# Attention rows in turns of two differential and two grouped-query rows, with the second map folded in by the ratio of the sums

## The chip, the cores and the metric

The program runs on one core of one Trainium2 chip. The metric is the device time of one execution in microseconds. The engines are TensorE (PE; its weight loads are shown as PEld), VectorE (DVE), ScalarE (ACT), GpSimd (POOL) and SyncE (SP). All DMAs of this kernel are issued from SP's queue. The 16 DMA engines of the core do the transfers, and also the transposes of 16-bit tiles (DMA_TRANSPOSE), which are called turns below.

## The reference, cut to what matters

One layer of a hybrid block over 2048 latent tokens and 256 context tokens, width 1024. Three mixers run side by side: pooling, differential attention (4 heads, two maps each) and grouped-query attention (8 heads of 64, two key/value groups of 4 heads). Queries are the 2048 latent tokens; keys and values are all 2304 tokens.

```
def _diff_core(q, k, v, lam):
    s = einsum('bqhcd,bkhcd->bhcqk', q, k) * (DIFF_HEAD_DIM ** -0.5)
    p = softmax(s, axis=-1)
    a = p[:, :, 0] - lam * p[:, :, 1]
    return einsum('bhqk,bkhe->bqhe', a, v)

def _diff_post(o, diff_subln, lam_init):
    o = _rmsnorm(o, diff_subln) * (1.0 - lam_init)

def _gqa_core(q, k, v):
    s = einsum('bqgrd,bkgd->bgrqk', q, k) * (GQA_HEAD_DIM ** -0.5)
    p = softmax(s, axis=-1)
    return einsum('bgrqk,bkgd->bqgrd', p, v)
```

Around it stand one input projection, gates (SiLU paths and sigmoid merges), branch projections and an output projection.

## The kernel before, in words

There are three stages. Stage 1 makes normalised tokens, projects queries, keys and values, and rounds them to pairs of f16 (a high part and what it leaves, a low part) in DRAM. Its fourth projection (the loop with `gating`) also loads the last third of `ada_w` through the `raw` tag and adds its products (`ada_product`, line 218), two per token tile. Stage 3 merges the branches and projects to the output.

Stage 2, which the change is about, has 256 score rows (line 710). A row is 128 queries of one map against all 2304 tokens. `score_row` issues ten matmuls in two PSUM tiles `sa` (1024 columns) and `sb` (1280), takes the maxima on VectorE (lines 759 to 761) and the exponentials on ScalarE with their sums (lines 764, 765). The PSUM tiles exist once, so the matmuls of the next row wait for the exponentials of this one. The first 128 rows are differential: for each head h and block j of 256 queries, halves o = 0, 1, and in each the maps c = 0, 1. The last 128 rows are grouped-query (gqa): 8 heads, 8 blocks, two halves.

What follows a row is put in two tables: `ahead` (issued before the scores of a slot) and `after` (issued behind them). For a pair of differential rows with the second at slot i: at i+1 the inverse sums, a GpSimd pass that scales the second map (`scale_second`, line 802), and VectorE's `combine` (line 806); at i+2 `high`, the f16 part on ScalarE, and `low`, the rest on VectorE (line 815). A gqa row does `high` (line 833) and `low` (line 838) at i+1. Each of them ends in `turn`: a DMA_TRANSPOSE of 128 x 2304 values into the tile `th` (line 786). Parts have four buffers, maps (`pt`) three, turned tiles four, for two steps at once. A step is a block of 256 queries; when both halves are turned, `diff_av` (54 matmuls of 256 columns) or `gqa_av` (36) multiplies it with the values, from the table `fills`: two rows after its last `low`.

PE's remaining time in a slot is filled with the gate projection (`gate_unit`, 24 matmuls of 512 columns for one 128 x 512 tile, 160 units). A planner at lines 928 to 960 gives each row the same PE time: it counts 1.95 for a row, 0.107 for an av matmul, 0.2135 for a gate matmul, and takes av work first, then gate matmuls, until the slot's goal is reached. Units 0 to 15 go out as they are, units 16 to 63 (SiLU paths) get a tanh on ScalarE and then the VectorE step of line 189, units 64 and up a tanh only. Gate weights come through the tag `raw` and are split on GpSimd (lines 158 to 163). Values are loaded in six parts and split on VectorE (lines 742, 744), one part in two rows as a rule. `diff_norm` makes the inverse norms of all four heads at slot 136.

The engines work in the order in which the program issues to them, SP included: a DMA that waits holds up those behind it.

## Time and profile before

| | us |
|---|---|
| median of 3 runs (lowest to highest) | 3084.66 (3082.51 to 3088.21) |
| the profiled execution | 3082.73 |
| its span, first to last instruction | 3080.9 |
| PE busy in the span | 2830.0 (92%) |
| DVE busy | 2312.8 (75%) |
| ACT busy | 1561.5 (51%) |
| POOL busy | 858.7 (28%) |
| stage 2, first to last row's first reduction | 652.6 to 2530.8 |

Busy shares are means over stages with different limits. Matmuls overlap and their ends are modelled, so a busy PE is not PE at its peak. In the list of groups a line has the source line, engine, operation, tiles and shapes, the count, the busy time and the mean of one, and after the last bar the idle time of the engine just before, with what ended it.

### The profile page before, as it was taken

The numbers are of one execution on the slowest core, as the hardware profiler recorded it, in microseconds if no ns is written. First come the engines' busy times: TensorE is split into PE (matmuls) and PEld (weight loads), VectorE is DVE, ScalarE is ACT, GpSimd is POOL, SyncE is SP. The second block draws the span as 40 slices with busy tenths as digits, with TensorE's granted clock in tenths as the row PEclk, the third lists the DMA queues.
The fourth block names the chain that finished last, engine by engine and source line by source line (L and its number), as shares of the span: only waits on it lengthen the run. The fifth ranks groups of instructions, "written<-read, shape, count | busy, mean of one in ns | idle before, by whom it ended". The sixth has DMA issues, their size and how long they took to land. (4 is left out here: it accounts for less than half of the span.)

```text
span 3080.9 us, 40994 instructions
## 1 busy us (share of the span) xinstructions
PE 2830.0 (92%) x15013; PEld 1656.3 (54%) x15013; DVE 2312.8 (75%) x2886; ACT 1561.5 (51%) x2038; POOL 858.7 (28%) x752
## 2 busy tenths in 40 slices
PE   6997887899999999999998998998999997999999
PEld 1543333645545545545555555555555554787787
DVE  3567885668988988988987887888788775756753
ACT  4722121236556556556666776777777772223221
POOL 0034453533332332332322010010010113434421
PEclk8999998999999999999999999999999998999999
DMA  6243552246666765666689999999999997677574
GB/s 238 103 123 100 140 144 62 64 109 138 149 142 132 149 145 128 154 137 146 145 178 174 200 196 199 196 195 197 203 197 198 196 193 218 209 253 250 201 256 150
DMA packets 1134266, 516.46 MB, mean 168 GB/s; under 512 B 985040, under 2 KB 1038704, under 8 KB 1134064
## 3 DMA queue, kind: packets, MB, share of 16 engines
q1 hardware_dynamic: 1134064, 513.84, 70.4%
q8 instruction: 118, 1.93, 0.2%
q14 instruction: 84, 0.69, 0.1%
HBM read 208.24 MB, written 78.97 MB: 93 GB/s over the span
## 5 line engine op out<-in xcount | busy, mean ns | idle before, releaser
L177 PE MATMUL gate<-hT,gws 128*128 128x512 f16 x3840 | 872.5, 381 | 0.0
L177 PEld LDWEIGHTS <-gws 128*128 128x128 f16 x3840 | 374.3, 98 | 421.7 <-issue 21.0
L764 ACT ACTIVATE pt<-sa,nm,escale 128x1024 f32<-128x1024 f32 x256 | 307.9, 1203 | 439.7 <-DVE nm L761 392.3
L756 PEld LDWEIGHTS <-qt 128*128 128x128 f16 x2560 | 249.9, 98 | 337.6 <-issue 52.2
L838 DVE SCALAR_TENSOR_TENSOR lo<-pt,nm,hi 128x2304 f16<-128x2304 f32 x128 | 339.0, 2649 | 101.2 <-DMA th<-lo 92.9
L491 PE MATMUL qkv<-wt,hT 128*128 128x512 f16 (+1 forms) x1920 | 400.1, 365 | 0.0
L760 DVE TENSOR_REDUCE nm<-sb 128x1 f32<-128x1280 f32 x256 | 379.0, 1480 | 0.6 <-PE sb L756 0.6
L833 ACT ACTIVATE hi<-pt,nm 128x2304 f16<-128x2304 f32 x128 | 283.5, 2215 | 177.9 <-DMA th<-hi 121.9
L878 PE MATMUL av<-th,vt 128*128 128x256 f16 x2304 | 287.9, 284 | 85.9 <-DMA th<-lo 46.7
L759 DVE TENSOR_REDUCE nm<-sa 128x1 f32<-128x1024 f32 x256 | 311.1, 1215 | 73.3 <-PE sa L756 72.5
L765 ACT ACTIVATE pt<-sb,nm,escale 128x1280 f32<-128x1280 f32 x256 | 360.4, 1408 | 0.0
L756 PE MATMUL sb<-kt,qt 128*128 128x512 f16 (+1 forms) x1536 | 319.2, 344 | 13.7 <-ACT pt L765 12.9
L878 PEld LDWEIGHTS <-vt 128*128 128x128 f16 x2304 | 229.6, 102 | 140.5 <-issue 63.6
L162 POOL TENSOR_SCALAR gws<-gw 128x512 f16<-128x512 f32 x76 | 76.5, 1006 | 812.4 <-PE gate L177 808.0
L491 PEld LDWEIGHTS <-hT 128*128 128x128 f16 x1920 | 191.4, 100 | 182.2 <-issue 18.2
L756 PE MATMUL sa<-kt,qt 128*128 128x512 f16 x1024 | 262.9, 379 | 12.8 <-ACT pt L764 5.7
L802 POOL TENSOR_SCALAR pt<-pt,nm,neglam 128x2304 f32<-128x2304 f32 x64 | 144.7, 2261 | 459.7 <-DVE nm L771 437.4
L1125 PE MATMUL br<-bt,wt 128*128 128x512 f32 x1152 | 268.2, 393 | 2.4 <-DVE wt L980 2.4
L1125 PEld LDWEIGHTS br<-bt,wt 128*128 128x128 f32 x1152 | 217.4, 189 | 52.0 <-DVE wt L980 3.5
L852 PE MATMUL av<-th,vt 128*128 128x256 f16 x1728 | 198.9, 273 | 1.1 <-ACT ms L868 1.1
L1157 PE MATMUL out<-y,wt 128*128 128x512 f32 x768 | 187.3, 403 | 9.9 <-DVE wt L980 4.7
L378 ACT ACTIVATE sp<-tpq 128x512 f16<-128x512 f32 (+1 forms) x68 | 34.8, 512 | 313.0 <-PE tpq L376 310.4
(195 smaller groups left out, 3323.0 us busy)
## 6 DMA issues: line engine op xcount, KB each, us to landing
tD<-gt SPq DMA_DIRECT2D x96, 256.0 KB, 2.4
wr<-in_w_br SPq DMA_DIRECT2D x32, 768.0 KB
ld<-tD SPq DMA_DIRECT2D x96, 256.0 KB, 4.6
scan<-in_w_gate SPq DMA_DIRECT2D x40, 512.0 KB, 3.9
gw<-in_w_gate SPq DMA_DIRECT2D x80, 256.0 KB, 4.0
qt<-qD SPq DMA_DIRECT2D x256, 64.0 KB, 2.7
wr<-in_w_out SPq DMA_DIRECT2D x32, 512.0 KB, 4.3
sgD<-gt SPq DMA_DIRECT2D x48, 256.0 KB, 2.4
```

The source lines that it names most:

```text
L177: nc.tensor.matmul(ps, lhsT=w[:, b, k, :], rhs=hT[k][:, a, c * CH:(c + 1) * CH], start=(n == 0), stop=(n == 3 * KT - 1))
L491: nc.tensor.matmul(ps[:, :width], lhsT=tokens_of(t, k, a), rhs=wt[k][:, b, :width], start=(n == 0), stop=(n == 3 * KT - 1))
L756: nc.tensor.matmul(dst, lhsT=qt[:, s, o * P:(o + 1) * P], rhs=kt[:, k0:k1], start=(s == 0), stop=(s == 1))
L759: nc.vector.tensor_reduce(out=nm[:, 0:1], in_=sa, axis=AX.X, op=ALU.max, negate=True)
L760: nc.vector.tensor_reduce(out=nm[:, 1:2], in_=sb, axis=AX.X, op=ALU.max, negate=True)
L764: nc.scalar.activation(out=pt[:, :SA], in_=sa, func=AF.Exp, scale=escale[:, m:m + 1], bias=nm[:, 0:1], accum_out=nm[:, 2:3])
L765: nc.scalar.activation(out=pt[:, SA:], in_=sb, func=AF.Exp, scale=escale[:, m:m + 1], bias=nm[:, 0:1], accum_out=nm[:, 3:4])
L833: nc.scalar.activation(out=box["hi"], in_=pt, func=AF.Copy, scale=nm[:, 2:3])
L838: nc.vector.scalar_tensor_tensor(out=lo, in0=pt, scalar=nm[:, 2:3], in1=box["hi"], op0=ALU.mult, op1=ALU.subtract)
L852: nc.tensor.matmul(ps[:, :256], lhsT=vt[:, k, v, :], rhs=pts[a][:, k, :], start=(n == 0), stop=(n == 3 * NKT - 1))
L878: nc.tensor.matmul(ps[:, :256], lhsT=vt[:, k, :, :].rearrange("p a d -> p (a d)"), rhs=pts[a][:, k, :], start=(n == 0), stop=(n == 2 * NKT ...
L1125: nc.tensor.matmul(ps, lhsT=wb[:, a, 4 * br + k, :], rhs=branch_tile(c, br, k)[:, b], start=(m == 0), stop=(m == 11))
```

## The change

The rows run in turns: two differential rows, two gqa rows, and so on, so that eight rows hold one differential step and two gqa steps. `high` and `low` of a gqa row stand two slots after its scores, and its av work at i+4. The second map is no longer scaled on GpSimd: `combine` multiplies it by (sum of the first) / (sum of the second) x (-lambda) while it adds the first map, and the common inverse sum is applied in `high` and `low`. Values of a differential head have one buffer, gqa values two; both are loaded two parts per slot from the third row of a head on (or two slots before a group). `diff_norm` runs once for each head, twelve rows into the next head, and for the last head behind all rows. The `raw` tag has 4 buffers instead of 5, maps 4 instead of 3, query tiles 5 instead of 4; the ada products of stage 1 follow their loads by one token tile instead of two. Forced av work is now counted by the planner.

```diff
     def raw(name):
-        return shp.tile([P, 512], F32, name=name, tag="raw", bufs=5)
+        return shp.tile([P, 512], F32, name=name, tag="raw", bufs=4)
...
-                if gating and u < 10:
+                if gating and u < 9:
...
-                        if m >= 4:
-                            ada_product(gps[m % 2], (m - 4) // 2, ada_raws.pop(0))
-                elif gating and u == 10:
+                        if m >= 2:
+                            ada_product(gps[m % 2], (m - 2) // 2, ada_raws.pop(0))
+                elif gating and u == 9:
                     rws = ada_rows(gps)
...
-        rows = [("d", h, j, o, c) for h in range(4) for j in range(8) for o in range(2) for c in range(2)]
-        rows += [("g", h, j, o, 0) for h in range(8) for j in range(8) for o in range(2)]
+
+        rows = []
+        for n in range(32):
+            for o in range(2):
+                rows += [("d", n // 8, n % 8, o, c) for c in range(2)]
+                m = 2 * n + o
+                rows += [("g", m // 8, m % 8, p, 0) for p in range(2)]
...
             if part == 0:
-                values[key] = sp.tile([P, NKT, 2, n], F16, name="vt", tag="vt", bufs=2)
+
+                use_up((key[0], key[1] - 1))
+                values[key] = sp.tile([P, NKT, 2, n], F16, name="vt", tag="vt" + key[0], bufs=1 if key[0] == "d" else 2)
...
-            pt = sp.tile([P, NTOK], F32, name="pt", tag="pt", bufs=3)
+            pt = sp.tile([P, NTOK], F32, name="pt", tag="pt", bufs=4)
...
-            nc.vector.reciprocal(out=nm[:, 2:3], in_=nm[:, 2:3])
+            nc.vector.reciprocal(out=nm[:, 3:4], in_=nm[:, 2:3])
...
-            def scale_second():
+            def ratio():
+
                 inverse_sum(nm, lscale[:, 0:1])
-                nc.gpsimd.tensor_scalar(out=pt, in0=pt, scalar1=nm[:, 2:3], scalar2=neglam[:, 0:1], op0=ALU.mult,
-                                        op1=ALU.mult)
+                nc.vector.tensor_scalar(out=nm[:, 2:3], in0=nm[:, 3:4], scalar1=n0[:, 2:3], scalar2=neglam[:, 0:1],
+                                        op0=ALU.mult, op1=ALU.mult)
 
             def combine():
-                nc.vector.scalar_tensor_tensor(out=p0, in0=p0, scalar=n0[:, 2:3], in1=pt, op0=ALU.mult, op1=ALU.add)
+                nc.vector.scalar_tensor_tensor(out=p0, in0=pt, scalar=nm[:, 2:3], in1=p0, op0=ALU.mult, op1=ALU.add)
...
-                nc.scalar.activation(out=box["hi"], in_=p0, func=AF.Copy)
+                nc.scalar.activation(out=box["hi"], in_=p0, func=AF.Copy, scale=n0[:, 3:4])
...
-                nc.vector.tensor_tensor(out=lo, in0=p0, in1=box["hi"], op=ALU.subtract)
+                nc.vector.scalar_tensor_tensor(out=lo, in0=p0, scalar=n0[:, 3:4], in1=box["hi"], op0=ALU.mult,
+                                               op1=ALU.subtract)
...
-            at(ahead, i + 1, high)
-            at(after, i + 1, low)
+            at(ahead, i + 2, high)
+            at(after, i + 2, low)
             if o == 1:
-                at(fills, i + 3, lambda: gqa_av(h, j, values["g", h // 4], turned.pop(step)))
+                at(fills, i + 4, lambda: (("g", h // 4), gqa_av(h, j, values["g", h // 4], turned.pop(step))))
...
-        def diff_norm():
-
-            rr = sp.tile([P, 64], F32, name="rr", tag="rr", bufs=1)
-            for h in range(4):
-                dma(out=rr[:, h * 16:(h + 1) * 16], in_=msD[h].rearrange("o (p t) -> p (o t)", p=P))
+        def diff_norm(h):
+
+            rr = sp.tile([P, 16], F32, name="rr", tag="rr", bufs=2)
+            dma(out=rr, in_=msD[h].rearrange("o (p t) -> p (o t)", p=P))
...
+                if kind == "d":
+                    at(ahead, i - 3, lambda h=h, c=c: load_keys((h, c), h, c))
+                    if c == 0:
+                        for p in range(6):
+                            at(ahead, i + 3 + p // 2, lambda h=h, p=p: load_part(("d", h), vD, h * P, P, 0, p))
+                        if h:
+                            at(ahead, i + 12, lambda h=h: split_later.append(diff_norm(h - 1)))
+                elif h % 4 == 0:
+                    at(ahead, i - 2, lambda g=h // 4: load_keys(("g", g), 4, g))
                     for p in range(6):
+                        at(ahead, i - 2 + p // 2, lambda g=h // 4, p=p: load_part(("g", g), gvD, g * 64, 64, 1, p))
+        at(ahead, NR + 5, lambda: split_later.append(diff_norm(3)))
```

## Rows read from the trace of the kernel before

**Rows 1.** The page: span, and the busy tenths of 40 slices for DMA.

```profile
span 3080.9 us, 40994 instructions
DMA  6243552246666765666689999999999997677574
```

**Rows 2.** Busy time by stretch: us, each engine's busy us and instructions, clock, DMA share.

```profile
762.30:1337.80 575.50, 555.60 (x3122) 300.73 (x3121) 510.54 (x564) 337.53 (x450) 192.51 (x138) 1.00 0.65 142
1397.10:1560.30 163.20, 163.20 (x935) 90.19 (x934) 144.94 (x157) 101.20 (x135) 57.29 (x43) 1.00 0.65 146
1688.70:2530.80 842.10, 768.81 (x4534) 445.46 (x4533) 678.46 (x736) 601.84 (x670) 103.73 (x89) 0.98 1.01 197
```

**Rows 3.** The same stretches for line 759 alone: the count is that of rows.

```profile
762.30:1337.80 575.50, 96.61 (x80) 1.00 0.65 142
1397.10:1560.30 163.20, 29.33 (x24) 1.00 0.65 146
1688.70:2530.80 842.10, 135.26 (x112) 0.98 1.01 197
```

**Rows 4.** Instructions on tile sa: ns min/median/max, first and last start in us.

```profile
L759 DVE TENSOR_REDUCE nm<-sa x256: 1203/1223/1226, 652.6 to 2530.8; 128x1 f32<-128x1024 f32 x128
```

**Rows 5.** Groups of PE in the stretch 1397.1 to 1560.3.

```profile
L177 PE MATMUL gate<-hT,gws 128*128 128x512 f16 x360 | 80.7, 379 | 0.0
L852 PE MATMUL av<-th,vt 128*128 128x256 f16 x323 | 37.2, 273 | 0.0
L756 PE MATMUL sb<-kt,qt 128*128 128x512 f16 (+1 forms) x144 | 30.0, 343 | 0.0
L756 PE MATMUL sa<-kt,qt 128*128 128x512 f16 x96 | 24.6, 379 | 0.0
L866 PE MATMUL ms<-o,ones 128*1 128x256 f32 x12 | 3.6, 377 | 0.0
```

**Rows 6.** The chain of waits, pieces by time: start us, us, what.

```profile
2188.87 4.75 PE gate L177 x22
...
2195.56 3.71 PE av L878 x35
```

**Rows 7.** Groups of PE, DVE and ACT in the gqa stretch 1688.7 to 2530.8.

```profile
L177 PE MATMUL gate<-hT,gws 128*128 128x512 f16 x1404 | 322.8, 380 | 0.0
L878 PE MATMUL av<-th,vt 128*128 128x256 f16 x2016 | 248.9, 281 | 71.4 <-DMA th<-lo 43.9 <-DMA th<-hi 23.5 <-DVE nm L761 1.9
...
L838 DVE SCALAR_TENSOR_TENSOR lo<-pt,nm,hi 128x2304 f16<-128x2304 f32 x111 | 294.3, 2652 | 86.0 <-DMA th<-lo 79.8 <-ACT hi L833 5.8
...
L833 ACT ACTIVATE hi<-pt,nm 128x2304 f16<-128x2304 f32 x111 | 245.9, 2215 | 155.9 <-DMA th<-hi 105.1 <-DVE nm L771 39.4 <-DVE nm L761 3.2
```

**Rows 8.** Groups of DVE in the stretch with line 189, 762.3 to 1337.8.

```profile
L806 DVE SCALAR_TENSOR_TENSOR pt<-pt,nm 128x2304 f32<-128x2304 f32 x40 | 105.6, 2641 | 2.5 <-POOL pt L802 2.5
...
L189 DVE SCALAR_TENSOR_TENSOR gt<-gt,gate 128x512 f32<-128x512 f32 x48 | 32.9, 686 | 42.2 <-ACT gt L186 42.2
...
L769 DVE TENSOR_SCALAR nm<-nm,lscale 128x1 f32<-128x1 f32 x80 | 21.5, 269 | 7.6 <-ACT pt L765 7.6
```

**Rows 9.** The hardware DMA queue: 1688.7 to 2530.8, then 1397.1 to 1560.3.

```profile
q1 hardware_dynamic: 554098, 165.36, 100.4%
...
q1 hardware_dynamic: 66268, 23.74, 64.9%
```

**Rows 10.** Instructions on tile th: issue of a turn on SP, and time to landing.

```profile
L786 SPq DMA_TRANSPOSE th<-lo x192: 2389/2748/3739, 679.5 to 2549.2; - x192
...
DMA to landing us min/median/max: 4.5/4.8/6.4
```

**Rows 11.** Timeline behind the last row: start us, us, what.

```profile
2559.25 17.00 PE L177 MATMUL gate<-hT,gws 128*128 128x512 f16 x78
```

**Rows 12.** Timeline in stage 1: an ada load, and the next product on PE.

```profile
456.26 0.89 SPq L667 DMA_DIRECT2D aw<-in_ada_w  x2
...
460.32 1.88 PE L218 MATMUL ada<-aw,cct 128*2 128x512 f32 x4
```

**Rows 13.** All splits of values on VectorE, ns min/median/max.

```profile
L744 DVE SCALAR_TENSOR_TENSOR vt<-vr,vscale,vt x36: 417/619/1559, 662.8 to 2026.1; 128x384 f16<-128x384 f32 x24, 128x192 f16<-128x192 f32 x12
```

More of the change, by code (lines that the diff above doesn't have):

```diff
@@ L725, in load_queries @@
         def load_queries(key, pair, half, j):
-            qt = queries[key] = sp.tile([P, 2, 256], F16, name="qt", tag="qt", bufs=4)
+            qt = queries[key] = sp.tile([P, 2, 256], F16, name="qt", tag="qt", bufs=5)
             for o in range(2):
@@ L778, in turn @@
                 while a == 0 and len(live) == 2:
-                    for _ in avs[0]:
-                        pass
-                    avs.pop(0)
+                    finish_first()
                 if a == 0:
@@ L822, in diff_row @@
             if o == 1:
-                at(fills, i + 4, lambda: diff_av(h, j, values["d", h], turned.pop(step)))
+                at(fills, i + 4, lambda: (("d", h), diff_av(h, j, values["d", h], turned.pop(step))))
         def gqa_row(i, h, j, o):
@@ L866, in square_sum @@
                 nc.tensor.matmul(pm[0:1, :256], lhsT=ones, rhs=o2, start=True, stop=True)
-                ms = sp.tile([1, 256], F32, name="ms", tag="ms", bufs=1)
+                ms = sp.tile([1, 256], F32, name="ms", tag="o2", bufs=2)
                 nc.scalar.activation(out=ms, in_=pm[0:1, :256], func=AF.Copy)
@@ L898, in rest @@
                 nc.vector.tensor_scalar(out=rr, in0=rr, scalar1=1.0 / P, scalar2=EPS, op0=ALU.mult, op1=ALU.add)
-                nc.gpsimd.tensor_tensor(out=rr, in0=rr, in1=mhalf, op=ALU.pow)
-                for h in range(4):
-                    dma(out=rD[h].rearrange("o (p t) -> p (o t)", p=P), in_=rr[:, h * 16:(h + 1) * 16])
-            return rest
-        fills, first = {}, {}
+                nc.gpsimd.tensor_tensor(out=rr, in0=rr, in1=mhalf[:, :16], op=ALU.pow)
+                dma(out=rD[h].rearrange("o (p t) -> p (o t)", p=P), in_=rr)
@@ L906, in block_kernel, with load_part @@
+            return rest
+        fills, first, split_later = {}, {}, []
+        def load_part(key, src, c0, n, m, p):
+            split_later.append(load_values(key, src, c0, n, m, p))
         for i, (kind, h, j, o, c) in enumerate(rows):
-            if kind == "d":
-                if j == 0 and o == 0:
-                    at(ahead, i - (5 if c == 0 else 1) if h else 0, lambda h=h, c=c: load_keys((h, c), h, c))
-                if o == 0:
-                    at(ahead, i - 3, lambda h=h, c=c, j=j: load_queries((h, j, c), h, c, j))
-                if j == 0 and o == 0 and c == 0:
-                    for p in range(6):
-                        at(ahead, i + p - 1 if h == 0 else i - 14 + 2 * p, lambda h=h, p=p: split_later.append(
-                            load_values(("d", h), vD, h * P, P, 0, p)))
-            else:
-                g = h // 4
-                if h % 4 == 0 and j == 0 and o == 0:
-                    at(ahead, i - 20, lambda g=g: load_keys(("g", g), 4, g))
-                    for p in range(6):
-                        at(ahead, i - 16 + 2 * p, lambda g=g, p=p: split_later.append(
-                            load_values(("g", g), gvD, g * 64, 64, 1, p)))
-                if o == 0:
-                    at(ahead, i - 4, lambda h=h, j=j: load_queries((4 + h, j, 0), 4 + h // 2, h % 2, j))
@@ L925, in block_kernel @@
-        split_later = []
-        at(ahead, 136, lambda: split_later.append(diff_norm()))
+            if o == 0:
+                pair = (h, c) if kind == "d" else (4 + h // 2, h % 2)
+                key = (h, j, c) if kind == "d" else (4 + h, j, 0)
+                at(ahead, i - 3, lambda key=key, pair=pair, j=j: load_queries(key, *pair, j))
+            if j == 0 and o == 0:
+                if kind == "d":
[7 more added lines that the diff above has]
+                    at(ahead, i - 2, lambda g=h // 4: load_keys(("g", g), 4, g))
+                    for p in range(6):
+                        at(ahead, i - 2 + p // 2, lambda g=h // 4, p=p: load_part(("g", g), gvD, g * 64, 64, 1, p))
@@ L928, in block_kernel @@
+        at(ahead, NR + 5, lambda: split_later.append(diff_norm(3)))
         total = (160 - HEAD_UNITS - TAIL_UNITS) * 24 * 0.2135 + NR * 1.95 + 32 * (54 * 0.107 + 0.45) + 64 * 36 * 0.107
-        spent = 0.0
+        spent = [0.0]
         row_now = [0]
-        for i in range(NR + 5):
+        for i in range(NR + 7):
             row_now[0] = i
@@ L945, in block_kernel @@
                     gqa_row(i, h, j, o)
-                spent += 1.95
+                spent[0] += 1.95
             for f in todo + after.pop(i, []):
                 f()
-            goal = total * (i + 1) / NR if i < NR else spent + 24 * 0.2135 * (i < NR + 3)
-            while avs and spent < goal:
-                t = next(avs[0], None)
+            goal = total * (i + 1) / NR if i < NR else spent[0] + 24 * 0.2135 * (i < NR + 4)
+            while avs and spent[0] < goal:
+                t = next(avs[0][1], None)
                 if t is None:
@@ L954, in block_kernel @@
                 else:
-                    spent += t
-            while spent < goal:
+                    spent[0] += t
+            while spent[0] < goal:
                 t = next(dense, None)
@@ L959, in block_kernel @@
                     break
-                spent += t
-        for a in avs:
+                spent[0] += t
+        for _, a in avs:
             for _ in a:
                 pass
+        assert not (ahead or after or fills)
     if stop == 2:
```

12 lines of the change are left out of this document (9 added, 3 removed).

## The prediction

> **What bounds the kernel now.** I began with the page's forty slices. The DMA line stands at 9 from about 1600 us to 2540 us and at 5 to 7 in the 900 us before that [rows 1]. Both halves are the attention stage, of 256 score rows, 128 differential rows and then 128 grouped-query (gqa) rows. So the next view was busy time by stretch, with the count of the row's first reduction in the same stretches as a row counter [rows 2, 3]. It gives three paces: 575.5/80 = 7.19 us a row while gate tiles with the extra VectorE step (line 189) are made, 163.2/24 = 6.80 us for differential rows without that step, and 842.1/111 = 7.59 us for gqa rows. All 255 steps from the first row's reduction to the last take 2530.8 - 652.6 = 1878.2 us [rows 4].
>
> Is 6.80 a floor? PE is busy in all 163.2 us of its stretch, but the matmuls overlap, so that alone says little. I took the pitch instead: 22 gate matmuls in a row are 4.75 us, 0.216 each, and 35 av matmuls 3.71 us, 0.106 each [rows 6]. With the counts of the stretch [rows 5] this is 360 x 0.216 + 323 x 0.106 + 96 x 0.216 + (96 x 0.216 + 48 x 0.106) + 3.6 = 162 of 163.2 us. PE streams without a hole there; 6.80 is its floor. The same sum for the gqa stretch, with the counts in its rows and 111 times the ten score matmuls, is 6.60 us a row, so 0.99 us a row is lost there. PE itself waits 71.4 us before the av matmuls, nearly all for a DMA turn (lo or hi being transposed into th); VectorE waits 79.8 us and ScalarE 105.1 us for the same turns, to get a buffer back [rows 7]. The granted clock is also a little lower, 0.98 against 1.00 [rows 2]. The hardware queue fills 100.4% of the 16 engines' time in the gqa stretch and 64.9% in the differential one [rows 9]. A gqa row sends two turns, a differential row one on average. In engine time a gqa row costs 1.004 x 7.59 = 7.62 us and a differential one 0.649 x 6.80 = 4.41 us; one turn is the difference, 3.2 us, and everything else 1.2 us a row. Thus gqa rows are bound by DMA, rows of the plain differential stretch by PE, rows with line 189 by a VectorE-ScalarE chain close to PE.
>
> **Part 1, the order.** In eight rows there will be four of each kind: twelve turns instead of eight or sixteen, 1.5 a row. DMA then needs 1.2 + 1.5 x 3.2 = 6.0 us a row, below the 6.80 of PE. PE's work is the same and is dealt out evenly by the planner: 3480 gate matmuls, 4032 av matmuls, 256 score rows and 32 square sums are 1695 us by the pitches above, 6.62 us a row. The slot in which each part runs shows bunching: three rows in succession carry two turns each (7.62 us of DMA each), the fourth none. A burst runs 3 x 0.8 = 2.4 us behind and the empty row gives it back. A turn lands 4.8 us after its issue [rows 10], and its av work comes two rows after the lo pass, so most of this lag is covered, though not surely the third row's. For rows without line 189 the ends are the floor 6.62 and the gqa pace of 7.59; I take 6.90, near the 6.80 that was reached with DMA under 100%, plus 0.1 for late turns. Rows with line 189: the 48 such tiles are units 16 to 63, and as gate work is dealt out a little more slowly in the first half they fall on about 83 rows, not 80. The wait of line 189 for ScalarE's tanh, 42.2 us [rows 8], stays as it is. I keep 7.19, with 7.05 and 7.3 as ends. Sum: 83 x 7.19 + 172 x 6.90 = 596.8 + 1186.8 = 1783.6 us.
>
> The page "Perfetto Trace Analysis" of the Trainium skill (Identifying the Most-Contended Engine) speaks against this part: it judges DMA by the memory's bandwidth and calls the occupancy of 16 engines misleading. By its 358 GB/s, the 197 GB/s of the gqa stretch would leave the DMA at 55%, and the part would gain nothing; that is the second rival below. Here the rows with waits for turns decide for me, and the same page's section What "DMA-bound" means allows the engines themselves to be the limit.
>
> **Part 2, the second map by the ratio.** The GpSimd pass over the second map goes. VectorE's combine waited for it 2.5 us in 40 times [rows 8], so on the path this is almost nothing. Added is one 128x1 step in each pair, about as long as the 0.27 us of line 769 [rows 8], and lo becomes the form that gqa rows use, 2.65 us [rows 7]. VectorE is busy 144.94/24 = 6.04 us a row now [rows 2]; with 0.14 and a few hundredths more it stays under 6.80. Where line 189 runs the 0.27 us lies in the chain in a quarter of the rows; I cost it at nothing, because gqa rows lose their wait for the sum in return (part 3), and the upper end 7.3 pays for it.
>
> **Part 3, gqa parts a row later.** high and low of a gqa row move to the second row after its scores. Then the inverse sum no longer waits for the exponentials just made, and the ScalarE wait on it, 39.4 us in 111 rows [rows 7], goes; it was not on PE's path. Queued behind these steps are only the next row's reductions and exponentials. Map buffers are held a row longer, and the fourth one covers that. The av work still comes two rows after low, as before. At the end the last map is turned a row later, two passes (2.2 and 2.65 us) that the remaining gate work covers: 78 gate matmuls, 17.0 us, stand there now [rows 11].
>
> **Part 4, loads.** Values are loaded and split two parts a row instead of one in two rows, so three rows in succession get 2 x 2 VectorE steps of 0.62 us [rows 13], 2.5 us, against some 0.7 us of slack. The load of the next part waits in SP's queue for these splits, with the turns of that row behind it. That is up to 1.8 x 3 = 5.4 us an event, in six events (four heads, two groups), 32 us; the present paces already hold some of it. I take 20, ends 8 and 32. The raw tag with 4 instead of 5: gate weights are asked for a little later, on SP's queue, cover is a column of 24 x 4 matmuls, nothing (upper end some 10 us if turns wait behind it). In the projection stage each ada product follows its load by one tile, not two: issued at 456.26, needed from 460.32 [rows 12], about the time of a landing; ends 0 and 7 us, I take 2. The normalisation of the last head now stands at the stage's end on SP: two short round trips ahead of the next stage's loads, under the 17.0 us of gate work [rows 11]; ends 0 and 6, I take 2.
>
> **Sum.** 1783.6 + 20 - 1878.2 + 2 + 2 = -70.6 us. The profiled execution took 3082.73 us (span 3080.9), so 3012; the median of the runs is 1.9 us above it. I predict 3013.
>
> **Rivals.** First, bursts still bind in part: the third row's turns are late in half the steps, rows without line 189 take 7.15, with it 7.25: 1229.8 + 601.8 + 30 = 1861.6, some 3070. For it: SP needs 2 x 2.75 us to issue two turns [rows 10], so a burst row leaves it about 1.3 us for all else. Second, slower: a gqa step (two rows and their av) keeps what it costs over the plain pace, 2 x 0.79 = 1.58 us, because the delay is that of two turns for each of two successive rows and not of the average load; the bursts keep just that. Then 83 x 7.19 + 172 x 6.80 + 64 x 1.58 + 32 = 1899, and with 9 us at the ends some 3112. It turns slower from about 1.3 us a step. Against it: waits of this kind need a full queue, and the empty rows drain it. Third, more gain: the waits vanish and the later gqa parts loosen the line 189 chain too: 172 x 6.72 + 83 x 7.05 + 8 = 1749, some 2955. For it: PE's own work is 6.62 us a row, and PE streamed without a hole at 6.80. Fourth, no change: the first and second in a mixture, some 3082.
>
> **How the numbers follow.** Forecast (2985 to 3040) 0.62; bursts bind in part (to about 3076) 0.15; more gain 0.12; no change 0.04; slower 0.07. A measurement of this kernel can tell about 0.2% from no change, 6 us. So faster is 0.62 + 0.15 + 0.12 = 0.89, same 0.04, slower 0.07. The range 2970 to 3055 holds the forecast, half of the more-gain case and two thirds of the burst case, about 0.8.
>
> **What would show it.** Right: DMA slices near 8 or 9 all through the stage instead of 6 and then 9; rows at about 6.9 us after the line 189 stretch; waits for th before av under a third of 71 us; granted clock near 1.00. Wrong: av waits on the step whose lo falls in a burst's third row, rows of 10 us and more; several slow rows each time values are loaded; a hole of PE before the first pool matmul of the last stage.

## The result, and the profile after

The changed kernel takes 3001.23 us, median of its runs (2999.54 to 3005.09), against 3085.05 us before: a ratio of 0.973, 95% interval 0.9713 to 0.9746. The forecast was 3013 us, between 2970 and 3055. The gain is 84 us where 72 were forecast.

In the page of the changed kernel DMA is busy at 7 to 9 all through the attention stage, where before it stood at 5 to 7 and then at 9 [rows 1]. Span, then the slices of DMA:

```profile
span 2997.8 us, 40968 instructions
DMA  6233543238888888789899898899997986677674
```

The next two views of the changed kernel answer to [rows 2, 3]: busy time by stretch (us, each engine's busy us and instructions, clock, DMA share, GB/s), and the same stretches for the first reduction of a row, now line 766, as a counter. Each stretch begins and ends with a reduction, so the row at its end is counted too.

```profile
774.40:1352.00 577.60, 552.72 (x3194) 310.34 (x3193) 509.94 (x579) 388.61 (x466) 93.93 (x83) 1.00 0.85 173
1461.50:1569.30 107.80, 107.80 (x640) 62.07 (x638) 95.60 (x106) 77.14 (x93) 13.68 (x14) 1.00 0.90 181
1687.30:2013.80 326.50, 323.67 (x1915) 186.18 (x1914) 286.99 (x314) 231.77 (x279) 45.94 (x47) 1.00 0.90 181
```

```profile
774.40:1352.00 577.60, 96.94 (x81) 1.00 0.85 173
1461.50:1569.30 107.80, 19.48 (x17) 1.00 0.90 181
1687.30:2013.80 326.50, 58.55 (x49) 1.00 0.90 181
```

Rows with line 189 take 577.6/80 = 7.22 us, one head change (4.6 us, below) among them; rows without it 107.8/16 = 6.74 us, and 326.5/48 = 6.80 us where one long row is among them. There is no row kind left that takes 7.59 us. PE is busy in all 107.8 us of the second stretch, and the clock is 1.00 in all three. PE's groups in that stretch, as in [rows 5]:

```profile
L177 PE MATMUL gate<-hT,gws 128*128 128x512 f16 x221 | 50.0, 379 | 0.0
L763 PE MATMUL sb<-kt,qt 128*128 128x512 f16 (+1 forms) x99 | 20.7, 345 | 0.0
L763 PE MATMUL sa<-kt,qt 128*128 128x512 f16 x64 | 16.4, 379 | 0.0
L894 PE MATMUL av<-th,vt 128*128 128x256 f16 x144 | 16.4, 273 | 0.0
L868 PE MATMUL av<-th,vt 128*128 128x256 f16 x108 | 12.4, 273 | 0.0
L882 PE MATMUL ms<-o,ones 128*1 128x256 f32 x4 | 1.2, 377 | 0.0
```

By the pitches of the prediction, with ten score matmuls in each of the 16 rows, this is 106.7 of 107.8 us, or 6.67 us a row. PE streams here too, and a row holds a little less work than the plain rows of before, which had 162/24 = 6.75 us.

All rows from the first reduction to the last, in the view of that line's instructions (answers to [rows 4]), then the groups of the av matmuls: gqa av in the whole run, from the page, and in the stretch 1687.3 to 2013.8 (answers to [rows 7]); then the hardware queue in the stretches 774.4 to 1352.0 and 1687.3 to 2013.8 (answers to [rows 9]):

```profile
L766 DVE TENSOR_REDUCE nm<-sa x256: 1204/1217/1227, 660.7 to 2444.4; 128x1 f32<-128x1024 f32 x128
```

```profile
L894 PE MATMUL av<-th,vt 128*128 128x256 f16 x2304 | 262.6, 273 | 8.2 <-DMA th<-hi 5.4
...
L894 PE MATMUL av<-th,vt 128*128 128x256 f16 x432 | 49.3, 273 | 2.8 <-DMA th<-hi 2.5 <-DMA th<-lo 0.3
```

```profile
q1 hardware_dynamic: 306457, 99.25, 84.3%
...
q1 hardware_dynamic: 181259, 58.88, 89.4%
```

The waits of PE for turns before av work went from 71.4 us in the gqa stretch alone [rows 7] to 8.2 us in the whole run. DMA's need in the mixed rows is 0.894 x 6.80 = 6.1 us a row.

The span fell by 3080.9 - 2997.8 = 83.1 us. Its parts: first to last row's reduction 1878.2 to 1783.7, that is -94.5; the first reduction at 660.7 instead of 652.6, +8.1; what follows the last reduction 550.1 to 553.4, +3.3. The last two come from one execution of each kernel, and executions of the same code scatter by some us there (the numbers are with the ada experiment and with the account of the prediction).

**The two ends.** Behind the last rows, the timeline of PE, POOL and SP shows the short chain of the last head's normalisation and the hole of PE ahead of the first pool matmul (start us, us, what, idle before it in brackets); the last line is the first pool matmul of the kernel before:

```profile
2473.78 15.71 PE L177 MATMUL gate<-hT,gws 128*128 128x512 f16 x72
2495.20 2.06 PE L1084 MATMUL mix<-pl,pw 128*128 128x512 f32 x3 [5.71 <-POOL s L1062]
...
2477.19 2.91 POOL L914 TENSOR_TENSOR rr<-rr,mhalf 128x16 f32<-128x16 f32 x1 [12.96 <-DVE rr L913]
...
2480.13 0.32 SPq L915 DMA_DIRECT2D rD<-rr  x1
2481.64 0.34 SPq L1180 DMA_DIRECT2D pse<-in_pool_edge  x1
...
2576.75 0.49 PE L1068 MATMUL mix<-pl,pw 128*128 128x512 f32 x1 [0.50 <-ACT pl L979]
```

The first load of the last stage stands in SP's queue behind the store of `rr`, which waits for 2.91 us of GpSimd. The hole is 5.7 us; before it was 0.5 us. In the projection stage, the waits of PE between 420 and 520 us (what is waited for, us in all, times, longest) have a line that the same stretch of before has not:

```profile
PE ada L218 <- DMA aw<-in_ada_w: 2.9, 1, 2.9
```

**Long rows.** From the starts of line 766, the four head changes stand out: rows 4 to 6 take 8.40, 9.36 and 7.71 us, rows 68 to 70 take 9.69, 9.00 and 8.31, rows 128 to 134 hold one of 10.97 and one of 9.11, rows 196 to 198 take 8.40, 8.40 and 8.45. Over their neighbours this is 5.3 + 4.6 + 10.5 + 5.0 = 25 us. A few single rows of 8.6 to 9.7 us stand elsewhere. Rows 196 to 198 by stretch, VectorE being the third engine:

```profile
2040.40:2065.70 25.30, 23.28 (x117) 11.01 (x116) 24.83 (x32) 14.49 (x18) 5.98 (x5) 1.00 0.91 192
```

VectorE is busy in 24.83 of the 25.30 us. In a plain row it is busy 95.60/16 = 5.98 us of 6.74; four split steps add some 2.4 us, 8.4 in all, and that is the pitch of these rows.

### The profile page after: what moved, and what is told of

Read it like the earlier page. It is cut to its first block, busy times and chain, and to the rows that moved or that the text cites. A ratio compares the mean times of both kernels' runs of the same rounds, so it can differ in the third digit from the quotient of the medians.

```text
span 2997.8 us, 40968 instructions
## 1 busy us (share of the span) xinstructions
PE 2800.9 (93%) x15013; PEld 1650.1 (55%) x15013; DVE 2322.5 (77%) x2953; ACT 1569.1 (52%) x2040; POOL 706.5 (24%) x689
## 5 line engine op out<-in xcount | busy, mean ns | idle before, releaser
L894 PE MATMUL av<-th,vt 128*128 128x256 f16 x2304 | 262.6, 273 | 8.2 <-DMA th<-hi 5.4
L878 POOL TENSOR_TENSOR o<-ot 128x256 f32<-128x256 f32 x32 | 22.0, 687 | 841.5 <-ACT ot L874 799.4
L868 PE MATMUL av<-th,vt 128*128 128x256 f16 x1728 | 198.9, 273 | 0.0
```

Source lines behind the costliest of these rows:

```text
L894: nc.tensor.matmul(ps[:, :256], lhsT=vt[:, k, :, :].rearrange("p a d -> p (a d)"), rhs=pts[a][:, k, :], start=(n == 0), stop=(n == 2 * NKT ...
```

## The experiments

The theory was that of the prediction: gqa rows had been bound by two turns a row on DMA, and the order averages this load, so that PE's floor comes in sight. The rivals were that another part of the change brought the gain, or that bursts or VectorE set the new pace. "Rows" below are pitches from one row's first reduction to the next. Ratios are to the kernel before, which was run beside each of these kernels; 0.973 is that of the changed kernel.

**Old order, all else as changed.**

```diff
-        rows = []
-        for n in range(32):
-            for o in range(2):
-                rows += [("d", n // 8, n % 8, o, c) for c in range(2)]
-                m = 2 * n + o
-                rows += [("g", m // 8, m % 8, p, 0) for p in range(2)]
+        rows = [("d", h, j, o, c) for h in range(4) for j in range(8) for o in range(2) for c in range(2)]
+        rows += [("g", h, j, o, 0) for h in range(8) for j in range(8) for o in range(2)]
```

> The changed kernel with the old order of rows (128 differential, then 128 gqa); all its other parts stay. Theory (the order does it, because DMA work per row is evened out): the gqa half goes back to some 7.6 us a row, the differential half to about 6.75 and 7.15, so 3001 + 128 x 0.85 = some 3100 us (3080 to 3115). Rival (the parts loosen the row: gqa parts a row later, fourth map buffer, no GpSimd pass): stays under 3025 us.

3116.0 us, ratio 1.0088 (1.007 to 1.0105), 1 us above the range expected. The stretch of gqa rows by stretch, its row counter, its queue and PE's waits in it:

```profile
1704.40:2550.32 845.92, 768.72 (x4514) 443.39 (x4512) 673.72 (x734) 601.32 (x671) 94.24 (x84) 0.98 1.01 197
...
1704.40:2550.32 845.92, 135.29 (x112) 0.98 1.01 197
...
q1 hardware_dynamic: 553940, 166.02, 100.9%
...
PE av L890 <- DMA th<-lo: 39.7, 41, 2.9
PE av L890 <- DMA th<-hi: 30.2, 25, 2.8
```

845.92/111 = 7.62 us a row, a full queue, and 69.9 us of waits for turns: all as before [rows 3, 7, 9], though gqa parts are made a row later here and the fourth map buffer is there. From the first reduction to the last it is 1893.8 us, so with all else as changed the order is worth 1893.8 - 1783.7 = 110 us, and what else was changed costs 15.6 us in the old order. Part of that is seen: with one buffer for the values of a head, each head change holds a row of 13.00 us and, two rows on, three of 8.1 to 10.3.

**One turn less in a gqa row of the kernel before.**

```diff
                 nc.vector.scalar_tensor_tensor(out=lo, in0=pt, scalar=nm[:, 2:3], in1=box["hi"], op0=ALU.mult,
                                                op1=ALU.subtract)
-                turn(lo, step, 1, o)
...
-rhs=pts[a][:, k, :], start=(n == 0), stop=(n == 2 * NKT - 1))
+rhs=pts[0][:, k, :], start=(n == 0), stop=(n == 2 * NKT - 1))
```

> The kernel before, but the low part of a gqa row is not turned, and the high part is multiplied twice in its place: every engine but DMA does the same work, a gqa row sends one turn instead of two. Theory (gqa rows are bound by the 16 engines' time): DMA need falls from 7.6 to 4.4 us a row, gqa rows come to 6.7 to 6.8 us, 3085 - 128 x 0.83 = some 2980 us (2965 to 2995). Rival (the delay of a single turn behind its part, not the load): the waits for hi stay, at most half goes, 3030 us or more.

2968.05 us, ratio 0.9608 (0.9594 to 0.9623). The gqa rows in the same views:

```profile
1686.00:2427.62 741.62, 740.46 (x4535) 443.46 (x4533) 671.51 (x734) 603.83 (x670) 116.67 (x89) 1.00 0.64 135
...
1686.00:2427.62 741.62, 134.65 (x111) 1.00 0.64 135
...
q1 hardware_dynamic: 294249, 99.69, 64.0%
```

The kernel leaves the low parts of the gqa maps out of its result. 741.62/111 = 6.68 us a row instead of 7.59, with the same work on PE, VectorE and ScalarE; PE has no hole left. This shows that the second turn is the cause of the slow gqa rows. It also measures a turn: 1.004 x 7.59 - 0.640 x 6.68 = 3.3 us of all 16 engines, where the prediction had taken 3.2 from a difference of two stretches. What it can't tell is how much of the bound was SP's, which issues a turn in 2.75 us [rows 10]: the durations of SP's DMA instructions add up to 95% of the gqa stretch of before and to 61% here, where the queue's share goes from 100.4% [rows 9] to 64.0%. The fuller queue speaks for the engines; it is not shown.

The rule of the Trainium skill weighed in the prediction ("Perfetto Trace Analysis", Identifying the Most-Contended Engine: judge DMA by the memory's bandwidth) would have called 197 of 358 GB/s no bound. This run disagrees: fewer turns alone made the rows 0.91 us shorter. The 197 GB/s count all that the DMA engines moved, so the memory's own share was no larger than that. The same sentence of that page of the Trainium skill goes on to ask which DMA resource binds, and that half agrees with a queue at 100.4%.

**Coarser turns: four and four, sixteen and sixteen rows.**

```diff
-        for n in range(32):
-            for o in range(2):
-                rows += [("d", n // 8, n % 8, o, c) for c in range(2)]
-                m = 2 * n + o
-                rows += [("g", m // 8, m % 8, p, 0) for p in range(2)]
+        for n in range(0, 32, 1):
+            rows += [("d", b // 8, b % 8, o, c) for b in range(n, n + 1) for o in range(2) for c in range(2)]
+            rows += [("g", m // 8, m % 8, p, 0) for m in range(2 * n, 2 * n + 2) for p in range(2)]
```

For sixteen and sixteen the three ranges are `range(0, 32, 4)`, `range(n, n + 4)` and `range(2 * n, 2 * n + 8)`.

> The changed kernel with four differential rows, then four gqa rows, and so on: the same twelve turns in eight rows, but five rows in succession with two turns each. Theory (average load, and a lag that two rows of slack cover): five times 0.85 us is 4.2 us of lag, just inside the slack, so 3001 to 3020 us. Rival (a row of two turns is late by itself): the five rows each lose about 0.8 us, 32 x 4 = some 3100 us.

3033.26 us, ratio 0.982 (0.9803 to 0.9836).

> The changed kernel with sixteen differential rows, then sixteen gqa rows: the average load is the same, but sixteen rows in succession need 16 x 0.85 = 13.6 us more of DMA than PE's pace gives, far more than two rows of buffers cover. Theory: about 9 us lost in each of the eight groups, 3070 us (3050 to 3090), with waits for turns back in the gqa rows. Rival (the parts loosen the row, the order matters not): 3001 to 3010 us.

3072.9 us, ratio 0.9946 (0.9931 to 0.9962). Sixteen and sixteen came out as expected of buffers that bridge a few rows only; four and four fell between its two expectations. In turns of four the undisturbed rows take 6.82 us instead of 6.74, and two thirds of the loss, some 22 of 33 us between the first row and the last, lie at the head changes, with rows of 10.7, 14.5 and 13.8 us; what the bursts have to do with those is not shown. In turns of sixteen, the blocks of gqa parts take 7.1 to 7.3 us a row, rows of 9 to 12 us among them, and the queue is nearly full in such a block (last but one number):

```profile
1476.00:1595.00 119.00, 113.80 (x671) 65.77 (x670) 97.70 (x105) 85.04 (x98) 15.02 (x15) 0.99 0.97 190
```

So the load is averaged over a few rows only, and the first rival of the prediction (bursts bind) is right for longer bursts than this change makes. That it is the four buffers of the parts and of the turned tiles that set how many rows is argued, not shown.

**gqa parts at the old distance, order as changed.**

```diff
-            at(ahead, i + 2, high)
-            at(after, i + 2, low)
+            at(ahead, i + 1, high)
+            at(after, i + 1, low)
             if o == 1:
-                at(fills, i + 4, ...
+                at(fills, i + 3, ...
```

> The changed kernel with high and low of a gqa row one row after its scores and its av work at i+3, as before the change. Then in every fourth slot the parts of a differential pair and of a gqa row fall together, four turns and two lo passes, and other slots have none. Theory (moving the gqa parts a row later is what deals the passes out one to a slot): the slots with two lo passes take 2 x 2.65 + 3.1 = 8.4 us of VectorE against 6.75, about 1.5 us lost in a quarter of the rows, 3001 + 64 x 1.5 = some 3095 us (3050 to 3110). Rival (the later parts only take away a wait that was off the path, as the prediction had it): 3000 to 3015 us.

3223.19 us, ratio 1.0437 (1.0421 to 1.0453): 222 us slower than the changed kernel, and slower than before. The reading of the prediction, that this part is worth nothing, falls. One long row on the timeline, first ScalarE, then VectorE, then PE:

```profile
1837.71 2.21 ACT L825 ACTIVATE hi<-pt,nm 128x2304 f16<-128x2304 f32 x1
1839.81 2.21 ACT L849 ACTIVATE hi<-pt,nm 128x2304 f16<-128x2304 f32 x1
1842.05 0.47 ACT L902 ACTIVATE sh<-av,oscale 64x256 f32<-64x256 f32 x1
...
1842.56 0.48 DVE L903 SCALAR_TENSOR_TENSOR ot<-av,oscale,sh 64x256 f32<-64x256 f32 x1 [4.66 <-ACT sh L902]
1842.96 1.20 DVE L766 TENSOR_REDUCE nm<-sa 128x1 f32<-128x1024 f32 x1
...
1847.31 1.86 PE L763 MATMUL sa<-kt,qt 128*128 128x512 f16 x4 [3.10 <-ACT pt L771]
```

PE had made the scores of this row by 1839.9. But the differential pair and the gqa row now have their `high` in one slot, and two passes of 2.21 us stand on ScalarE ahead of `sh`; VectorE's step on `sh` stands ahead of the reductions and waits 4.66 us; PE then waits 3.10 us for the exponentials and the granted clock is 0.97 in the sixteen rows around it (1.00 in the changed kernel). Every eighth row takes 11.2 to 11.3 us in this kernel and the queue is at 78.3% there, so it is not DMA. The loss is more than twice the 94 us expected: the slots with two `low` passes are there, as the rows of 8.2 us behind the long ones, but the rows of 11.2 to 11.3 us were not foreseen. The later slot gives each of the three sets of parts a slot of its own. In the old order the edit shows nothing: gqa rows take 7.62 us with it and the other parts and 7.59 without them (first experiment). By itself it was not run in that order.

**The GpSimd pass put back.**

```diff
-                nc.vector.tensor_scalar(out=nm[:, 2:3], in0=nm[:, 3:4], scalar1=n0[:, 2:3], scalar2=neglam[:, 0:1],
+                nc.gpsimd.tensor_scalar(out=pt, in0=pt, scalar1=nm[:, 3:4], scalar2=neglam[:, 0:1], op0=ALU.mult,
...
-                nc.vector.scalar_tensor_tensor(out=p0, in0=pt, scalar=nm[:, 2:3], in1=p0, op0=ALU.mult, op1=ALU.add)
+                nc.vector.scalar_tensor_tensor(out=p0, in0=p0, scalar=n0[:, 3:4], in1=pt, op0=ALU.mult, op1=ALU.add)
```

> The changed kernel with the second map scaled by a GpSimd pass again, combine and the high and low parts of differential rows as they were. Theory (the ratio is worth almost nothing on the path): 2997 to 3010 us. Rival (combine's wait for the pass holds the chain of each second differential row): 1 us in each of 64 pairs, 3050 us or more.

3003.87 us, ratio 0.9729 (0.9712 to 0.9745), not to be told from the changed kernel's 0.973. The ratio of the sums is worth nothing that can be measured here, as the prediction had it.

**Values in smaller doses.**

```diff
-at(ahead, i + 3 + p // 2, lambda h=h, p=p: load_part(("d", h), ...
+at(ahead, i + 3 + p, lambda h=h, p=p: load_part(("d", h), ...
...
-at(ahead, i - 2 + p // 2, lambda g=h // 4, p=p: load_part(("g", g), ...
+at(ahead, (i - 8 if i > 8 else i - 2) + p, lambda g=h // 4, p=p: load_part(("g", g), ...
```

> The changed kernel with values loaded and split one part a row instead of two, from the third row of a head on, and for the second group eight rows ahead. Theory (the rows of 8.4 to 11 us behind each change of head are VectorE's four split steps a row): a row then has 1.25 us more VectorE work instead of 2.5, most of which fits; of some 27 us lost around the four changes 12 to 18 come back, 2985 us (2980 to 2992). Rival (what is lost there is SP's queue, which waits for the splits, or the load of keys): less than 6 us come back.

3008.95 us, ratio 0.9745 (0.9731 to 0.976): not faster, and the theory fell. The rows behind 68 are 8.73, 7.81, 7.14, 7.25, 7.82 and 7.62: smaller excesses, but six of them, in all 1.6 us less than in the changed kernel. Behind row 4 the same six rows take 3.2 us more, and at the group change rows of 11.22 and 10.39 us came up. So the doses make little difference. That the cost goes with the VectorE steps, and that spread out they hold the loads and turns behind them for longer, is argued, not shown by this run.

**The ada products two tiles behind their loads.**

```diff
-                if gating and u < 9:
+                if gating and u < 10:
...
-                        if m >= 2:
-                            ada_product(gps[m % 2], (m - 2) // 2, ada_raws.pop(0))
+                        if m >= 4:
+                            ada_product(gps[m % 2], (m - 4) // 2, ada_raws.pop(0))
```

> The changed kernel with the ada products of stage 1 again two token tiles behind their loads; raw keeps four buffers, so each product is issued ahead of the load that takes its buffer. Theory (the first row of stage 2 started 8 us later because the first product waited 2.9 us for its load, and the product that the shorter distance saves at the end is lost in the wait for the all-reduce): 2 to 6 us back, 2997 us; no wait of PE for ada loads in 420 to 520 us. Rival (the 8 us came from earlier in stage 1 and have nothing to do with it): 3001 us, no difference.

2996.75 us, ratio 0.9701 (0.9687 to 0.9715). The first row starts at 654.45 instead of 660.69, and PE no longer waits for `aw` between 420 and 520 us. So 6.2 of the 8.1 us at the start are the ada distance. One execution is not sure to a few us here: in the nine kernels with the shorter distance the first row starts between 656.6 and 660.7 us (mean 659.2), in the three with the longer one and four raw buffers between 651.4 and 654.5 (mean 652.8), in the two with the first stage of before at 652.6 and 654.1. By these means the distance is worth 6.4 us, and the other 1.9 us are within the scatter. Why a wait of 2.9 us grows to that stays open.

**Line 189 put off by a row.** In the changed kernel VectorE still waits for the tanh ahead of line 189, in the stretch 774.4 to 1352.0 as before [rows 8]:

```profile
L189 DVE SCALAR_TENSOR_TENSOR gt<-gt,gate 128x512 f32<-128x512 f32 x44 | 30.2, 687 | 37.0 <-ACT gt L186 36.8
```

```diff
-                nc.vector.scalar_tensor_tensor(out=gt, in0=gt, scalar=1.0, in1=ps, op0=ALU.add, op1=ALU.mult)
-                dma(out=sgD[c][i - 4], in_=gt)
+                def silu():
+                    nc.vector.scalar_tensor_tensor(out=gt, in0=gt, scalar=1.0, in1=ps, op0=ALU.add, op1=ALU.mult)
+                    dma(out=sgD[c][i - 4], in_=gt)
+                put_off[0](silu)
...
+        put_off[0] = lambda f: at(after, row_now[0] + 1, f)
```

> The changed kernel with the VectorE step of line 189 issued a row later, behind the next row's reductions, so that VectorE does not stand before ScalarE's tanh. Theory (rows with line 189 are 7.14 us and not 6.74 because the reductions queue behind this step, which waits for the exponentials and then the tanh): the stretch of 81 rows goes to 6.75 to 6.85 us, 25 to 30 us less, some 2973 us. Rival (VectorE's added busy time, 0.69 us a step, makes the rows longer): under 8 us less.

2984.61 us, ratio 0.9667 (0.9652 to 0.9681), less gain than expected. The rows with line 189 fell from about 7.15 to 6.8 us, but single rows of 12.56, 10.52 and 13.10 us came among them (rows 31, 77 and 87). The timeline of the first of these, VectorE, SP, ScalarE and PE:

```profile
865.60 0.68 DVE L191 SCALAR_TENSOR_TENSOR gt<-gt,gate 128x512 f32<-128x512 f32 x1
...
875.70 0.54 SPq L192 DMA_DIRECT2D sgD<-gt  x1
...
878.97 0.69 ACT L187 ACTIVATE gt<-gate,ginv 128x512 f32<-128x512 f32 x1 [6.35 <-DMA sgD<-gt]
...
883.00 1.14 PE L766 MATMUL sa<-kt,qt 128*128 128x512 f16 x4 [2.52 <-ACT pt L774]
```

The gate tile has two buffers. VectorE's step on it ends at 866.3, but its store is issued 9.4 us later, behind turns on SP; the next but one tanh waits 6.35 us for it, and the row's exponentials wait behind the tanh.

**The same, ahead of `low`, with the ada distance.**

```diff
-        put_off[0] = lambda f: at(after, row_now[0] + 1, f)
+        put_off[0] = lambda f: split_later.append(f)
```

The rest of the edit is that of the two experiments above.

> The changed kernel with the step of line 189 a row later, issued ahead of that row's low pass instead of behind it, and the ada products two tiles behind. Theory (the four rows of 9 to 13 us that the later step left were ScalarE's tanh waiting for the store of a gate tile, which stood behind a turn on SP's queue): the long rows go, rows with line 189 are at 6.75 us, 15 us less than with the step behind low, and 3 us from the products: some 2968 us (2962 to 2976). Rival (a third gate buffer is what is missing): the long rows stay, 2980 us.

2970.81 us, ratio 0.9621 (0.9607 to 0.9634): 30 us less than the changed kernel. Rows with line 189 take 6.75 us, as those without it, and the first row starts at 651.4. The expectation that the long rows go was a miss: 10.62, 10.00 and 11.20 us are left, in the same places. Two of them, rows 31 and 87, are as above: the tanh waits 4.20 and 3.08 us for the store of a gate tile. Row 77 is another case, which the theory did not have. VectorE's step on `rr`, for the norms of the head before, waits for its load and stands ahead of the step of line 189 (now L191) and of `low`:

```profile
1192.14 0.17 DVE L916 TENSOR_SCALAR rr<-rr 128x16 f32<-128x16 f32 x1 [3.16 <-DMA rr<-msD]
```

**Values split on GpSimd.**

```diff
-                nc.vector.tensor_scalar(out=vt[:, :, 0, :], in0=vr, scalar1=vscale[:, m:m + 1], scalar2=None,
-                                        op0=ALU.mult)
-                nc.vector.scalar_tensor_tensor(out=vt[:, :, 1, :], in0=vr, scalar=vscale[:, m:m + 1],
-                                               in1=vt[:, :, 0, :], op0=ALU.mult, op1=ALU.subtract)
+                nc.gpsimd.tensor_scalar(out=vr, in0=vr, scalar1=vscale[:, m:m + 1], scalar2=1.0, op0=ALU.mult, op1=ALU.mult)
+                nc.gpsimd.tensor_scalar(out=vt[:, :, 0, :], in0=vr, scalar1=1.0, scalar2=1.0, op0=ALU.mult, op1=ALU.mult)
+                nc.gpsimd.tensor_tensor(out=vt[:, :, 1, :], in0=vr, in1=vt[:, :, 0, :], op=ALU.subtract)
```

> The changed kernel with the values split by three GpSimd steps (scale, high part, rest) instead of two VectorE steps; loads and their slots stay. Theory A (what is lost at the four changes of head, some 27 us, is VectorE's time, of which the chain of a row has next to no slack): 15 to 22 us back, some 2983 us. Theory B (it is SP's queue, which waits for the splits before it can issue the next load and the turns behind it): under 6 us back, or worse, since GpSimd is slower, 2996 to 3010 us.

3001.68 us, ratio 0.9718 (0.9705 to 0.9732), and each theory had a part. Behind row 68 the rows are 7.86, 7.61, 6.95 (9.69, 9.00, 8.31 in the changed kernel): the VectorE steps were the cost there. But rows 7, 133 and 135 now take 12.39, 11.77 and 13.05 us. On the timeline of the last two, `high` on ScalarE and av on PE wait for turns:

```profile
1605.96 2.22 ACT L848 ACTIVATE hi<-pt,nm 128x2304 f16<-128x2304 f32 x1 [6.50 <-DMA th<-hi]
...
1623.52 3.79 PE L893 MATMUL av<-th,vt 128*128 128x256 f16 x18 [3.73 <-DMA th<-hi]
```

From 1585 to 1630 us SP's value loads wait 4.7 us for GpSimd's steps, where in the changed kernel (1590 to 1636) they wait 0.3 us for VectorE's. How much of the long rows this is, and how much the turns of this place, the run doesn't settle; the next one leaves the group changes alone.

**GpSimd splits for heads 1 and 3 alone, on top of the kernel with line 189 put off ahead of `low`.**

```diff
+                if key in (("d", 1), ("d", 3)):
+                    nc.gpsimd.tensor_scalar(out=vr, ...
...
+                else:
                     nc.vector.tensor_scalar(out=vt[:, :, 0, :], in0=vr, scalar1=vscale[:, m:m + 1], scalar2=None,
```

> The e10 kernel (2970.8 us in its own call), and only the values of differential heads 1 and 3 split by three GpSimd steps; heads 0 and 2 and both groups stay on VectorE. It tells apart what e11 left mixed. If the head changes cost VectorE time and GpSimd's splits are cheap as long as they do not meet a group's splits, the rows behind 64 fall from 9.4, 9.0, 8.3 to about 7.9, 7.6, 7.0 and those behind 192 from 8.4, 8.4, 8.5 to about 7.0, 6.7, 6.5, no new row of 10 us or more follows them, and the time is 2959 to 2966. If the GpSimd splits themselves hold up the turns in SP's queue, as behind row 128 in e11, new rows of 10 us or more stand within eight rows behind rows 64 and 192, and the time is 2969 or more. Also open and seen in the same run: whether the long rows of e10 (10.6 at row 31, 10.0 and 11.2 before row 96) stay; nothing is changed for them, so both theories say that they stay.

2970.35 us, ratio 0.9623 (0.9607 to 0.9638): no gain over 2970.81. Behind row 68 the rows are 6.74, 6.97 and 6.41 (9.44, 9.00, 8.31 in the kernel that it builds on), behind row 196 they are 6.95, 6.70 and 6.47: that cost is gone, as the first theory said. But row 71 now takes 11.34 us (6.97 there). On the timeline ahead of it, VectorE, GpSimd and SP, then SP, ScalarE and PE up to and in the row itself; the last line is SP's waits for value loads between 1105 and 1150 us:

```profile
1129.63 0.68 DVE L191 SCALAR_TENSOR_TENSOR gt<-gt,gate 128x512 f32<-128x512 f32 x1
1130.23 2.92 DVE L862 SCALAR_TENSOR_TENSOR lo<-pt,nm,hi 128x2304 f16<-128x2304 f32 x1
...
1130.71 2.89 POOL L753 TENSOR_SCALAR vr<-vr,vscale 128x384 f32<-128x384 f32 x1
...
1135.22 2.54 SPq L749 DMA_DIRECT2D vr<-vD  x2
...
1139.16 2.77 SPq L808 DMA_TRANSPOSE th<-hi  x1
1142.04 0.53 SPq L192 DMA_DIRECT2D sgD<-gt  x1
...
1144.75 0.69 ACT L187 ACTIVATE gt<-gate,ginv 128x512 f32<-128x512 f32 x1 [5.27 <-DMA sgD<-gt]
...
1143.89 3.08 PE L902 MATMUL av<-th,vt 128*128 128x256 f16 x18 [2.68 <-DMA th<-hi]
...
SPq L749 <- POOL vt L755: 4.0, 2, 2.3
```

In the row it is the picture of rows 31 and 87 of the two kernels above: a late store of a gate tile, a tanh that waits 5.27 us for the buffer, `high` and the exponentials behind the tanh. What made the store late is the second theory's mechanism in good part. The gate tile was ready at 1130.3. Its store is issued 11.7 us later, behind value loads, query loads and a turn, and SP's value loads waited 4.0 us there for GpSimd's splits (1.4 us for VectorE's in the kernel that it builds on). The first of these splits took 2.89 us where the median is 0.59, beside VectorE's `low`. Without the 4.0 us the tanh would have waited some 1.3 us, an estimate from these lines. Row 71 takes back 4.4 of the 11.8 us that the splits gave; row 79 and rows 199 to 204 take back another 5.2, and their causes were not traced. A third buffer for the gate tile was not tried, and the cause of these long rows rests on the timelines alone.

## Why the prediction was right

The sum was 1783.6 + 20 - 1878.2 + 2 + 2 = -70.6 us; the trace gives -83.1. Term by term:

- **What bounds the kernel.** DMA turns in gqa rows, PE in the plain differential rows: right, shown by taking one turn away (7.59 to 6.68 us a row) and by putting the old order back (7.62). DMA's need in the mix, 6.0 us forecast, is 0.894 x 6.80 = 6.1.
- **Rows without line 189.** 6.90 forecast, 6.74 measured: mis-sized by 172 x 0.16 = 27.5 us, the largest error. The 0.1 us for late turns is not there. The rest is that 6.80 was the floor of rows with 6.75 us of PE work; the mixed rows hold 6.67, nearer to the mean of 6.62 that the prediction itself gives. The rival of more gain had 6.72 for these rows.
- **Rows with line 189.** 7.19 forecast. Sixteen rows without a head change have means of 7.05 to 7.18, so the term holds to about 0.05, and the wait for the tanh stayed as said: 36.8 us in 44 times, before 42.2 in 48. That this wait is what sets these rows is shown by putting the step off: 6.75.
- **Values.** 20 us forecast (8 to 32), 25 measured. The reason given, 2.5 us of VectorE steps against some 0.7 us of slack, comes out: the rows are 1.7 us longer and VectorE is full in them. For heads 1 and 3 it is also shown by moving the steps to GpSimd; for the group changes it is not, since there the move brought other waits.
- **The ends.** 2 us forecast for the ada distance, 6.2 of the 8.1 measured at the start; inside its ends (0 to 7), but the value taken was too small. 2 us for the normalisation at the end, 3.3 measured in this execution (what follows the last reduction is 553.3 to 557.4 us in the nine kernels with turns of two and two, so 3 to 7); the hole that the prediction named as a sign is there (5.7 us, before 0.5), with GpSimd's 2.91 us in the chain. No run took the tail apart.
- **Part 2** at nothing: right; putting the GpSimd pass back gave 0.9729 against 0.973.
- **Part 3** at nothing: the step that failed, though it moved no number. The prediction asked which wait goes in the old order (ScalarE's for the inverse sum, off PE's path), and for that order nothing here speaks against it. It didn't ask what the new order would do without the part: two `high` and two `low` passes in one slot, 222 us. It had counted the turns of each slot, but with part 3 already in place.
- **Bursts.** The rival didn't come about at two and two rows; at sixteen and sixteen it does, with 0.9946 instead of 0.973, and at four and four (0.982) it has a part at most. The signs named for it were not all absent: one row of 10.97 us stands at the group change.

So the errors were -27.5 for the plain rows, +5 for values and +7.4 for the two ends; the remaining 2.6 are single long rows and rounding, less about 4 us for the rows with line 189. Together they make the 12.5 between sum and trace. That the total came out nearer than its largest term is luck: errors of both signs met. (3012 and 1.9 make 3014, not the 3013 forecast; nothing hangs on it.)

## What to carry to other kernels

Where one half of a stage is bound by DMA and the other by TensorE, put their rows in turns as fine as the dependences allow: the load was averaged over a few rows only, and turns of sixteen gave back most of the gain. When the order changes, list for each slot the passes of every engine that fall into it, not the load of one engine alone, and cost each other edit both ways, with the new order and with the old; the edit that the forecast had at nothing was worth 222 us in the new order. When a step is put off, follow its store too: behind a long transfer in the same queue it holds a buffer, and the next writer waits. When a step goes to GpSimd, look which loads wait for it.

## What the runs showed of the hardware

A turn of 128 x 2304 values costs 3.3 us of all 16 DMA engines (1.004 x 7.59 - 0.640 x 6.68); rows with the queue at 100.4% were held by turns at 197 GB/s, and at 0.90 PE ran without a hole. The order of one DMA queue passes waits on: a store of 0.53 us, behind value loads that waited 4.0 us for GpSimd and a turn of 2.77 us, held ScalarE for 5.27 us. VectorE's busy time added up: 5.98 us in a plain row and some 2.4 us of split steps made rows of 8.4 us, with VectorE busy in 24.83 of 25.30 us. GpSimd steps have a second, longer duration beside VectorE's long passes: in the attention stage of the last experiment 29 GpSimd steps took at least 1.5 us more than the shortest of their kind, and every one began inside a VectorE pass of 2.6 us or more (`combine` or `low`) and ended after it; a power of 128 x 16 values took GpSimd 2.91 us at the stage's end and 5.21 us beside such a pass.
